# New durations and lags in a hybrid layer's ordering model, and thirteen list schedules in place of three

## The chip, the cores and the metric

The kernel runs on one core of a Trainium2 chip. The metric is the device time of one launch in microseconds (us), the median of several executions. Beside the times stands the trace of one profiled execution.

## The reference

One layer for 4096 tokens of width 1024, in float32: a pre-norm, one input projection that feeds two groups of heads, a gate on each group, one output projection, the residual and a final RMSNorm.

```python
h = _rmsnorm(x, norm_w)
u = (h @ w_in).astype(f32)                    # 1024 -> 3216 columns
# gated linear attention: 4 heads, key dim 64, value dim 128
#   S_t = diag(a_t) S_{t-1} + k_t^T v_t ;  o_t = q_t S_t        (in chunks)
gla_out = rmsnorm_of_head(o) * gla_norm_w * silu(gg)
# RWKV-7: 8 heads of size 64, token shift on r, k, v, w, a
def step(S, inp):
    r_t, w_t, k_t, v_t, kk_t, a_t = inp
    sa = jnp.einsum('bhvk,bhk->bhv', S, -kk_t)
    S = (S * w_t[:, :, None, :]
         + sa[..., None] * (kk_t * a_t)[:, :, None, :]
         + v_t[..., None] * k_t[:, :, None, :])
    y = jnp.einsum('bhvk,bhk->bhv', S, r_t)
    return S, y
rwkv_out = (group_norm(y) + bonus) * silu(rg)
merged = jnp.concatenate([gla_out, rwkv_out], axis=-1)
x = x + merged @ w_out
return _rmsnorm(x, final_norm_w)
```

## The kernel before

The 4096 tokens are worked in 8 blocks of 512. Activations lie transposed, channels on the 128 partitions and tokens along the row. The input projection's columns are 29 weight tiles of 128 columns and a narrow one; each weight and each activation is split into two float16 parts, and a projection tile (`proj`) is three products of parts over 8 tiles of depth, 24 matmuls of 512 columns into one bank of PSUM. Weights are split once, written to DRAM (`wdr`), and loaded again for each block by SyncE's queue (SP) into small rings of buffers (`wr`, `wg`, `wo` in the trace: 4, 3 and 2 buffers).

**A unit of RWKV.** The 8 heads are 4 pairs; pair times block makes 32 units. For each, `rwkv_ab` projects k, r, v and the gate, mixes in the shifted token, forms the decays, and takes the norm of k (`bones` matmuls on `rn`). Eight chunks of 64 tokens get their scores in 16 matmuls (`bank<-DD,bk`), which `copy_predicated` masks into `DD` and `Nb`. The delta rule needs the inverse of a triangular 64x64 matrix for each head and chunk. Its 32x32 diagonal blocks go through DRAM (`nd`) to a layout in which a partition holds a whole block (`f`), and 31 links of two instructions on GpSimd (POOL) invert 128 blocks at once:

```python
for j in range(31):
    m, w = j // 4 + 1, 31 - j
    E.tensor_tensor(tm[:, :m, :w], ..., ALU.mult)               # tm<-Tc,f
    E.tensor_tensor(Tc[:, :m, j + 1:], ..., tm[:, :m, :w], ALU.add)   # Tc<-Tc,tm
```

(The last unit's links run on VectorE.) The result goes back through DRAM (`td`) into `Nb`. `rwkv_i` transposes one half (`Ta`, on VectorE) and completes the 64x64 inverse by two sets of small matmuls (`bank<-Ta,Nb` is the first). `rwkv_c` then walks the state through 8 links of three matmuls (`ch<-sv,DD`, `ch<-us,Nb`, `ch<-uv,bk`) with copies by ScalarE and VectorE between them; `rwkv_d` norms and gates. The attention group runs beside this (`gla_proj`, `gla_pair`), and the output projection of a block (`out_block`, matmuls on `wo`) follows when both groups are done.

**What sets the order.** None of this is issued as it is written. Each engine is wrapped in `Engine`, and each call is recorded as a `Step` with its engine, duration, lag to its readers and what it depends on (all instructions so carry line 392 in the trace). Durations come from `cost` for VectorE ("V"), ScalarE ("S") and GpSimd ("G"), from column counts for TensorE ("T"), from bytes for DMAs ("D"). A first pass (`run`, with `account`) interleaves the streams of the program by priority and by the modelled times. Then `forward` makes a list schedule of all steps on the modelled engines, with a rank for each step; `backward` derives ranks from a schedule by going from its end to its start. `class Array` models TensorE: it charges changes of tile form, float32 passes and a slow clock after idleness. The schedules alternate, the one with the smallest modelled end is kept, and the steps are emitted in order of its start times, which gives each engine and SP's queue its order. Before, there are a first schedule, one from its ranks, and two more.

Of the kernel before, what the change touches and what calls it, by code (L numbers as in the profile page):

```python
# [25 lines left out]
SPARE = 0.45  # L26
# [55 lines left out]
def hymba_kernel(ctx, tc, xT, wt, wg, wo, wua, gup, pk, ck, out):  # L82
# [7 lines left out]
    big = ctx.enter_context(tc.tile_pool(name="big", bufs=1))  # L90
# [42 lines left out]
    class Array:  # L133
# [5 lines left out]
        def put(self, t, d, cols, tiles):  # L139
            r, c, f32 = tiles  # L140
            form = (r[1] - r[0], c[1] - c[0])
            q = [(i, j) for i in range(r[0], r[1]) for j in range(c[0], c[1])]
            turn = form != self.form
            t = max([t, self.free] + [self.tile.get(k, 0.0) for k in (self.tile if turn else q)]) + 0.09 * turn
            w, k = int(t / 3.413), self.clock
            if w > k[0]:
                k[:] = [w, 0.0, w == k[0] + 1 and k[1] >= 3060]
            k[1] += cols
            d *= 1 if k[2] else 2
            full = len(q) == 16  # L150
            if full and f32 == 2:
                d += (0.058 if cols <= 256 else 0.0) + (0.0 if self.f32 else 0.015)
            for k in q:
                self.tile[k] = t + (d if full or not f32 else 0.66 * d)
            self.form, self.f32 = form, f32 > 0
            self.free = t + (d if full or turn and f32 else d / 2 if f32 and form != (4, 1) else 0.014)
            return t, d
# [1 line left out]
    array = Array()  # L159

    def account(eng, out, ins, d, lag, cols=0, tiles=None):
        rdy = lambda k: (lambda r: r[0] - 0.1 if r[1] == eng and eng in "VSG" else r[0])(ready.get(k, (0.0, "")))
        t = max([0.0] + [rdy(k) for a in ins for k in parts(a)]
                + [used.get(k, 0.0) for k in parts(out)]
                + [rdy(k) for k in parts(out) if eng != "T"])
        if eng == "T":
            t0, d = array.put(max(t, now[0]), d, cols, tiles)
            t, now[0] = t0, array.free
        else:
            if eng == "D":  # L170
                t0 = place("H", t, 0.63)
                t = t0 + 1.28
            t = place(eng, t, d)
            if eng != "D":
                t0 = t
        for a in ins:
            for k in parts(a):
                used[k] = max(used.get(k, 0.0), t + d + (0.95 if eng == "D" else 0.1))
        for k in parts(out):
            ready[k] = (t + d + lag, eng)  # L180
        return t0

    table = [0]
    steps, wkey, rkey, wlast, readers = [], {}, {}, {}, {}
# [22 lines left out]
    def put(t0, eng, d, lag, cols, tiles, tab, outs, ins, f):  # L207

        keys = lambda aps: {k: k in {y for x in aps for y in parts(x)} for a in aps for k in whole(a)}
        ki, ko = keys(ins), keys(outs)  # L210
        for k in list(ki) + list(ko):
            t0 = max(t0, wkey.get(k, 0.0))
        for k in ko:
            t0 = max(t0, rkey.get(k, 0.0))
        s = Step(len(steps), t0, eng, d, lag, cols, tiles, tab, f)
        got = lambda m: m.lag + SPARE * (m.eng == "D") - 0.1 * (m.eng == eng and eng in "VSG")
        for k, timed in ki.items():
            rkey[k] = max(rkey.get(k, 0.0), t0)
            if k in wlast:
                s.follow(wlast[k], got(wlast[k]) if timed else None)  # L220
        for k, timed in ko.items():
            wkey[k] = t0
            if k in wlast:
                s.follow(wlast[k], got(wlast[k]) if timed and eng != "T" else None)
            for m in readers.get(k, ()):
                s.follow(m, (0.95 + SPARE if m.eng == "D" else 0.1) if timed else None)
            wlast[k], readers[k] = s, []
        for k in ki:
            if k not in ko:
                readers.setdefault(k, []).append(s)  # L230
        if eng == "T":

            if last[0] and last[1] == turn[0] and last[0].form == s.form != (4, 4):
                last[0].next = s
                s.follow(last[0], None)
            last[:] = [s, turn[0]]
        for m in s.on:
            m.to.append(s)
        steps.append(s)

    def forward(rank):


        wait, can, free = {e: [] for e in "VSGTD"}, {e: [] for e in "VSGTD"}, dict.fromkeys("VSGTDH", 0.0)
        pes, tab, run = Array(), 0, None
        left, ready, start = [len(s.on) for s in steps], [0.0] * len(steps), [0.0] * len(steps)
        end = [0.0] * len(steps)
        for s in steps:
            if not s.on:
                heapq.heappush(wait[s.eng], (0.0, s.n))  # L250

        def soonest(e):
            t = pes.free if e == "T" else free["H" if e == "D" else e]
            return t if can[e] else max(t, wait[e][0][0]) if wait[e] else 1e18

        for _ in steps:
            e = min("VSGTD", key=soonest)
            t = soonest(e)
            while wait[e] and wait[e][0][0] <= t:
                n = heapq.heappop(wait[e])[1]  # L260
                heapq.heappush(can[e], (rank[n], n))
            if e == "T":
                x = next((x for x in can[e] if run and x[1] == run.n), None)
                x = x or min(heapq.nsmallest(12, can[e]), key=lambda x: x[0] - 2.0 * (steps[x[1]].form == pes.form))
                run = steps[x[1]].next
                can[e].remove(x)
                heapq.heapify(can[e])
            else:
                x = can[e][0]
                soon = []  # L270
                while e in "VS" and wait[e] and wait[e][0][0] <= t + 0.15:
                    r, n = heapq.heappop(wait[e])
                    soon.append((r, n))
                    if rank[n] + 2 * (r - t) < x[0]:
                        x = (rank[n] + 2 * (r - t), n)
                for y in soon:
                    if y[1] != x[1]:
                        heapq.heappush(wait[e], y)
                if x is can[e][0]:
                    heapq.heappop(can[e])  # L280
            s = steps[x[1]]
            t, d = max(t, ready[s.n]), s.d
            start[s.n] = t
            if e == "T":
                start[s.n], d = pes.put(t, d, s.cols, s.tiles)
                end[s.n] = start[s.n] + d
            elif e == "D":
                free["H"], free["D"] = t + 0.63, max(t + 1.28, free["D"]) + d
                end[s.n] = free["D"]
            else:  # L290
                if s.tab is not None:
                    d, tab = d + 1.2 * (s.tab != tab), s.tab
                end[s.n] = free[e] = t + d
            for m in s.to:
                lat = m.on[s]
                ready[m.n] = max(ready[m.n], start[s.n] if lat is None or lat < 0 else end[s.n] + lat)
                left[m.n] -= 1
                if not left[m.n]:
                    heapq.heappush(wait[m.eng], (ready[m.n], m.n))
        return start, end  # L300
# [26 lines left out]
                    heapq.heappush(wait[m.eng], (ready[m.n], m.n))  # L327
        return [-t for t in late]

    def cost(eng, op, ins, n, o):  # L330

        big = [a for a in ins if math.prod(a.shape[1:]) > 1 or n == 1]
        few = len(ins) - len(big)
# [1 line left out]
        if eng == "V":  # L335
            fast = len(big) == 1 and not psum and op in ("tensor_scalar", "tensor_copy", "tensor_scalar_mul", "tensor_scalar_max")
            if op == "tensor_tensor_scan":
                return 0.068 + n / 480
            runs = 0.09 if n == 64 or len(o.shape) > 2 and o.shape[-1] == 64 and n == 512 else 0.0
            if op == "copy_predicated":  # L340
                runs = 0.09
            elif n == 256 and o.shape[0] != 128:
                runs += 0.04 if op == "transpose" else 0.09
            elif op == "tensor_scalar" and few > 1:
                runs = 0.06
            return 0.068 + 0.06 * (few > 0) + n / (1920 if fast else 960) + runs
        if eng == "G":
            return 0.225 + 0.07 * few + n * (2.13 if len(big) > 1 else 0.95) / 960
        return (0.1 if n == 64 and o.shape[0] == 64 else 0.0) + (0.052 if psum else 0.094) + n / 1200 + 0.09 * (few > 0)

    class Engine:

# [4 lines left out]
        def __getattr__(self, op):  # L357
            f = getattr(self.eng, op)

            def call(*a, **kw):  # L360
# [3 lines left out]
                if aps:  # L364
# [14 lines left out]
                    else:  # L379
                        e = kw.get("accum_out")  # L380
                        ins = [x for x in ins if x is not e]
                        outs = [o] + ([e] if e is not None else [])
                        d = cost(self.name, op, ins, n, o)
                        if op == "activation" and a[2] in (AF.Ln, AF.Exp, AF.Tanh):
                            tab = int(a[2] == AF.Ln)
                        load = 1.2 * (tab is not None and tab != table[0])
# [1072 lines left out]
    with tc.manual_schedule(engines={getattr(mybir.EngineType, e) for e in ("PE", "DVE", "Activation", "Pool", "SP")}):  # L1459
# [5 lines left out]
        run()  # L1465
        start, end = forward([s.t0 for s in steps])
        start, end = best = forward(backward(end))
        for _ in range(2):
            start, end = forward(backward(end))
            best = min(best, (start, end), key=lambda x: max(x[1]))  # L1470
        start, end = best
# [65 lines left out]
```

## Time and profile before

| | |
|---|---|
| median of 3 executions | 2358.89 us (2357.46 to 2363.66) |
| the profiled execution's own time | 2364.37 us |
| its span, first to last instruction | 2362.6 us |
| mean granted TensorE clock | 0.985 |
| DMA | 325.46 MB, mean 138 GB/s |

The page divides the span into 40 slices; a digit is the busy share of a slice in tenths.

```profile
PE   6889999999999999999999999999999999999997
DVE  6878877677764886756767678657876478676855
POOL 3351433526134152345322353332543435233400
PEclk9999999999999999999999999999999999999999
```

In the timelines a row is: start and duration in us, engine, line, operation, output and inputs by name, shape, count, and in brackets the idle time before it and what ended that.

### The profile page before, as it was taken

To read this page: it belongs to the slowest core of one execution; us is meant where nothing else is said; L and a number is where in the kernel's file an instruction comes from. 1 tells how busy PE (TensorE), PEld (TensorE's weight loads), DVE (VectorE), ACT (ScalarE), POOL (GpSimd) and SP (SyncE) were. 2 spreads that over 40 slices of the span, in tenths; PEclk is the share of its full clock that TensorE was granted. 3 is DMA by queue.
4 is the path that set the end of the run, shared out by engine and by line. 5 is a ranking of instruction groups with operands and counts; after the bars stand their busy time and mean duration, and the time that the engine had idled before them with its cause. 6 is when DMAs were issued, how large, how long until landed. Compare 5 with 4: busy or idle time off the path is not lost.

```text
span 2362.6 us, 52159 instructions
## 1 busy us (share of the span) xinstructions
PE 2250.2 (95%) x19432; PEld 1379.2 (58%) x19432; DVE 1679.0 (71%) x3737; ACT 1248.1 (53%) x3229; POOL 846.8 (36%) x2213
## 2 busy tenths in 40 slices
PE   6889999999999999999999999999999999999997
PEld 2556565556565656556575565755566556665564
DVE  6878877677764886756767678657876478676855
ACT  6557765454653554535554456445455465544442
POOL 3351433526134152345322353332543435233400
PEclk9999999999999999999999999999999999999999
DMA  6566554354334543335433444345533354334432
GB/s 190 178 217 200 186 164 153 115 169 146 100 94 142 174 150 84 110 119 182 141 96 110 152 153 133 90 124 180 152 101 106 124 183 142 97 111 124 141 82 93
DMA packets 275523, 325.46 MB, mean 138 GB/s; under 512 B 131732, under 2 KB 132932, under 8 KB 275268
## 3 DMA queue, kind: packets, MB, share of 16 engines
q1 hardware_dynamic: 275268, 322.13, 45.0%
q8 instruction: 152, 2.49, 0.4%
q14 instruction: 103, 0.84, 0.1%
HBM read 276.97 MB, written 45.05 MB: 136 GB/s over the span
## 4 chain that ended last, share of the span: by engine, by line
PE 63%; DVE 20%; ACT 6%; issue 4%; DMA 4%; POOL 3%; SPq 1%; DVEq 0%; ACTq 0%; POOLq 0%
PE bank L392 55%; PE ch L392 6%; DVE DD L392 3%; PE y L392 2%; DVE nta L392 2%; DVE bk L392 2%; DVE Nb L392 1%; POOL tm L392 1%; POOL Tc L392 1%; DVE mgg L392 1%; DVE mgr L392 1%; DMA xr<-in_xT_dram 1%; DMA rn<-bcda 1%; ACT gep L392 1%; DVE x L392 1%
## 5 line engine op out<-in xcount | busy, mean ns | idle before, releaser
L392 PE MATMUL bank<-x,wr 128*128 128x512 f16 x3264 | 806.8, 382 | 9.6 <-ACT x L392 2.8
L392 POOL TENSOR_TENSOR tm<-Tc,f 128x60 f32<-128x60 f32 (+24 forms) x961 | 332.5, 346 | 655.0 <-DMA f<-nd 535.5
L392 PEld LDWEIGHTS <-wr 128*128 128x128 f16 x3264 | 318.7, 100 | 308.0 <-issue 22.4
L392 PE MATMUL bank<-x,wg 128*128 128x512 f16 x1536 | 385.0, 381 | 5.6 <-DMA wg<-wdr 4.1
L392 POOL TENSOR_TENSOR Tc<-Tc,tm 128x60 f32<-128x60 f32 (+24 forms) x961 | 346.9, 361 | 73.7
L392 PE MATMUL bank<-x,wo 128*128 128x512 f16 x1488 | 357.0, 381 | 0.4 <-ACT bk L392 0.4
L392 DVE SCALAR_TENSOR_TENSOR sv<-ch,PC,psd 64x64 f32<-64x64 f32 x448 | 126.2, 282 | 213.4 <-PE ch L392 208.3
L392 POOL TENSOR_TENSOR xacc<-xacc,xr 128x512 f32<-128x512 f32 x98 | 130.6, 1332 | 335.4 <-ACT xr L392 237.9
L392 PEld LDWEIGHTS <-wg 128*128 128x128 f16 x1536 | 146.1, 100 | 149.7 <-issue 8.9
L392 PEld LDWEIGHTS <-wo 128*128 128x128 f16 x1488 | 144.9, 100 | 139.3 <-issue 4.1
L392 PEld LDWEIGHTS <-x 128*128 128x128 f16 x3120 | 187.5, 99 | 21.4 <-issue 6.8
L392 PE MATMUL bank<-wg,x 128*128 128x128 f16 x3072 | 196.1, 220 | 1.6 <-DMA wg<-wdr 0.8
L392 ACT ACTIVATE psd<-sv,PC 128x128 f32<-128x128 f32 x256 | 102.2, 399 | 178.3 <-DVE sv L392 139.1
L392 ACT COPY uv<-ch 64x64 f32<-64x64 f32 x512 | 105.4, 206 | 117.3 <-PE ch L392 112.5
L392 ACT COPY us<-ch 64x64 f32<-64x64 f32 x512 | 105.1, 205 | 103.8 <-PE ch L392 95.2
L392 POOL MEMSET Tc<- 32x8 f32 (+1 forms) x160 | 23.6, 148 | 302.9 <-DMA td<-Tc 280.2
L392 PEld LDWEIGHTS ch<-sv,DD 128*128 128x128 f32 x512 | 90.9, 192 | 52.1 <-DVE sv L392 25.0
L392 ACT ACTIVATE sa<-bank,mu_s 128x512 f32<-128x512 f32 x104 | 71.6, 689 | 88.7 <-PE bank L392 87.6
L392 PEld LDWEIGHTS ch<-uv,bk 128*128 128x128 f32 x512 | 90.2, 191 | 48.5 <-ACT uv L392 25.3
L392 PE MATMUL ch<-sv,DD 128*128 128x128 f32 x512 | 106.1, 289 | 12.3 <-DVE sv L392 10.9
L392 PEld LDWEIGHTS ch<-us,Nb 128*128 128x128 f32 x512 | 88.2, 192 | 44.1 <-ACT us L392 24.5
L392 PE MATMUL ch<-uv,bk 128*128 128x128 f32 x512 | 106.1, 289 | 6.3 <-ACT uv L392 5.9
(332 smaller groups left out, 3683.0 us busy)
## 6 DMA issues: line engine op xcount, KB each, us to landing
wr<-wdr SPq DMA_DIRECT2D x256, 256.0 KB
wg<-wdr SPq DMA_DIRECT2D x184, 256.0 KB
xr<-in_xT_dram SPq DMA_DIRECT2D x176, 256.0 KB
wo<-wdr SPq DMA_DIRECT2D x128, 256.0 KB
f<-nd SPq DMA_DIRECT2D x128, 128.0 KB
x<-in_wt_dram SPq DMA_DIRECT2D x29, 512.0 KB
wdr<-wo SPq DMA_DIRECT2D x25, 512.0 KB
out_dram<-mgg SPq DMA_DIRECT2D x33, 256.0 KB
```

The lines of the kernel that those rows point to most:

```text
L392: put(t0, self.name, d, lag, cols, tiles, tab, outs, ins, lambda: f(*a, **kw))
```

## The change

The code that computes is untouched; the model that orders it changes. `Array.put` charges more for a float32 matmul behind a float16 one, something for the reverse, and something for float32 matmuls of the form (2, 4). A new function `early` gives, for a pair of engines, by how much a result reaches its reader sooner than the common lag; it was 0.1 us on the same engine and nothing between engines, and is now different for each engine and pair. `cost` gets other constants for all three engines, among them GpSimd's start cost (0.225 to 0.14 us, and 0.34 more for 8 elements), half-height forms on VectorE, and short and half-height forms, several scalars and accumulation on ScalarE. A change of activation table costs 1.3 us in place of 1.2. The number of list schedules goes from 3 to 13 after the first. In the diff "V", "S", "G", "T" are VectorE, ScalarE, GpSimd, TensorE.

```diff
             if full and f32 == 2:
-                d += (0.058 if cols <= 256 else 0.0) + (0.0 if self.f32 else 0.015)
+                d += (0.058 if cols <= 256 else 0.0) + (0.0 if self.f32 else 0.045)
+            elif full and self.f32 and not f32:
+                d += 0.017
+            elif f32 and form == (2, 4):
+                d += 0.036
...
-        rdy = lambda k: (lambda r: r[0] - 0.1 if r[1] == eng and eng in "VSG" else r[0])(ready.get(k, (0.0, "")))
+        rdy = lambda k: (lambda r: r[0] + early(r[1], eng))(ready.get(k, (0.0, "")))
...
+    def early(a, b):
+        if a not in "VSGT" or b not in "VSGT" or not a:
+            return 0.0
+        if a == b:
+            return {"V": -0.075, "S": -0.1, "G": -0.18, "T": 0.0}[a]
+        return -0.045 if a == "T" else -0.09 if b == "T" else -0.07
...
-        got = lambda m: m.lag + SPARE * (m.eng == "D") - 0.1 * (m.eng == eng and eng in "VSG")
+        got = lambda m: m.lag + SPARE * (m.eng == "D") + early(m.eng, eng)
...
-                    d, tab = d + 1.2 * (s.tab != tab), s.tab
+                    d, tab = d + 1.3 * (s.tab != tab), s.tab
...
-    def cost(eng, op, ins, n, o):
+    def cost(eng, op, ins, n, o, acc=False):
...
-            runs = 0.09 if n == 64 or len(o.shape) > 2 and o.shape[-1] == 64 and n == 512 else 0.0
+            half = o.shape[0] < 128
+            runs = 0.0
             if op == "copy_predicated":
-                runs = 0.09
-            elif n == 256 and o.shape[0] != 128:
-                runs += 0.04 if op == "transpose" else 0.09
+                runs = 0.135 if half else 0.013
+            elif n == 64:
+                runs = 0.126
+            elif n == 256 and half:
+                runs = 0.122 if op == "transpose" else 0.09
+            elif n == 512 and half:
+                runs = 0.115
...
         if eng == "G":
-            return 0.225 + 0.07 * few + n * (2.13 if len(big) > 1 else 0.95) / 960
-        return (0.1 if n == 64 and o.shape[0] == 64 else 0.0) + (0.052 if psum else 0.094) + n / 1200 + 0.09 * (few > 0)
+            if op == "memset":
+                return 0.135 + n * 0.52 / 960
+            return 0.14 + 0.07 * few + n * (2.13 if len(big) > 1 else 0.95) / 960 + 0.34 * (n == 8)
+        if n <= 4:
+            return 0.1 if n == 1 else 0.03
+        if n == 64 and o.shape[0] == 64:
+            return 0.231 if psum else 0.147
+        d = (0.052 if psum else 0.094) + n / 1200 + 0.09 * (few > 0) + 0.11 * (o.shape[0] < 128)
+        return d + (0.035 + 0.05 * (few > 1) if few and psum and n > 128 else 0.02 * (few > 0)) + 0.1 * acc
...
-                        d = cost(self.name, op, ins, n, o)
+                        d = cost(self.name, op, ins, n, o, e is not None)
...
         start, end = best = forward(backward(end))
-        for _ in range(2):
+        for _ in range(12):
             start, end = forward(backward(end))
             best = min(best, (start, end), key=lambda x: max(x[1]))
```

## The prediction

> **What bounds the kernel now.** First the page: busy time, then the chain that ended last.
>
> ```profile
> PE 2250.2 (95%) x19432; PEld 1379.2 (58%) x19432; DVE 1679.0 (71%) x3737; ACT 1248.1 (53%) x3229; POOL 846.8 (36%) x2213
> PE 63%; DVE 20%; ACT 6%; issue 4%; DMA 4%; POOL 3%; SPq 1%; DVEq 0%; ACTq 0%; POOLq 0%
> ```
>
> TensorE works 2250.2 of the 2362.6 us span. No cost term and no lag changes what is computed, so that block stays: in the two compiled orders 14,756 matmul entries stand in each, and the array changes its tile form 2,139 times before and 2,141 after. Only the 2362.6 − 2250.2 = 112.4 us without TensorE work can move, and what matters is where they lie. The table by stage (columns: us of the stage, then busy us of PE, PEld, DVE, ACT, POOL, then clock, DMA share, GB/s):
>
> ```profile
> 0.00:300.00 300.00, 253.02 (x1997) 153.28 (x1997) 238.81 (x631) 195.54 (x405) 104.20 (x246) 0.95 0.62 194
> 300.00:2250.00 1950.00, 1905.07 (x16697) 1170.69 (x16695) 1374.72 (x2935) 1010.60 (x2703) 742.61 (x1967) 1.00 0.44 132
> 2250.00:2363.00 113.00, 92.09 (x745) 55.22 (x742) 65.46 (x173) 41.93 (x122) 0.00 (x0) 0.91 0.28 87
> ```
>
> The head loses 47 us, the long middle 45 (2.3%), the tail 21. Next, whom TensorE and SP's queue wait for (total, times, longest):
>
> ```profile
> PE bank L392 <- DVE bk L392: 12.9, 9, 6.8
> PE ch L392 <- DVE sv L392: 10.9, 13, 1.7
> PE bank L392 <- ACT wo L392: 6.8, 7, 2.1
> PE ch L392 <- ACT uv L392: 5.9, 11, 0.9
> PE bank L392 <- DMA wg<-wdr: 4.9, 4, 2.5
> PE bank L392 <- DVE Ta L392: 2.0, 2, 1.3
> SPq L392 <- POOL Tc L392: 101.4, 36, 6.8
> ```
>
> Many small waits, one of 6.8 us; and TensorE hardly ever waits for `Ta`, which comes out of POOL's inverse.
>
> **The change, term by term.** Every edit acts through the emitted order alone, so each is priced by what that order puts between a producer and its consumer. I compared the compiled orders of both kernels and turned the matmuls between two points into time by their columns, scaled to 2250.2 us in all. The median matmul moves 44 places of 24,516, VectorE's instructions 6, ScalarE's 5, SP's 3, POOL's 0.
>
> *Head.* The one long wait stands in TensorE's timeline:
>
> ```profile
> 59.21 0.43 PE L392 MATMUL bank<-rn,bones 128*32 128x128 f32 x8
> 59.57 4.49 PE L392 MATMUL bank<-x,wr 128*128 128x512 f16 x20
> ...
> 76.70 4.50 PE L392 MATMUL bank<-DD,bk 64*128 64x128 f32 x32 [6.82 <-DVE bk L392]
> 124.00 2.05 PE L392 MATMUL bank<-DD,bk 64*128 64x128 f32 x30 [0.27 <-DVE bk L392]
> 1007.80 2.97 PE L392 MATMUL bank<-x,wo 128*128 128x512 f16 x13
> ```
>
> From the norm sums (`rn,bones`) to the scores (`DD,bk`) lie 17.5 us, most of it a VectorE chain. The old order has 44 matmuls of 512 columns there (20 on wr, 24 on wg) and two small ones on `amW`; at 2.97/13 = 0.23 us each that is about 10 us, and then TensorE waits 6.82. In the new order the norm sums stand earlier, ahead of the low-rank matmuls, and 56 large matmuls and those small ones fill the stretch, about 12.9 us. If VectorE's chain keeps its length, the wait falls to some 2.5: −4.3. The 32 scores behind the wait took 4.50 us, 30 of a later unit 2.05; a shorter wait could give back part of these 2.3 us. Against both: 6.8 us of TensorE's waits are for `wo` still being split, and what comes sooner may wait there longer. I take −5, bounds −9 and 0. The Trainium skill ("TensorE: Matmul & The Clock Gate", § What's actually happening) says that an idle window of about 3.4 us halves the matmul clock; the 6.82 us wait with slow scores behind it agrees, and by it the whole 2.3 would come back and the term would be −6.6.
>
> *Weights.* Four weight loads have under 3 us of matmul columns between the freeing of their buffer and their first use in the old order, none in the new. The four waits for wg cost 4.9 us: −2, bounds −5 and 0.
>
> *POOL's inverse.* Here the model changes most. Each of 32 units has 31 links of two POOL instructions, and per unit the old constants (0.225, and a 0.1 lead) sum to 27.1 us, the new ones (0.14 and 0.34 for the link of 8 elements) to 22.5. The trace:
>
> ```profile
> L392 POOL TENSOR_TENSOR tm<-Tc,f 128x60 f32<-128x60 f32 (+24 forms) x961 | 332.5, 346 | 655.0 <-DMA f<-nd 535.5
> L392 POOL TENSOR_TENSOR Tc<-Tc,tm 128x60 f32<-128x60 f32 (+24 forms) x961 | 346.9, 361 | 73.7
> ```
>
> and from the timelines of POOL and VectorE, at two places:
>
> ```profile
> 517.88 0.72 POOL L392 TENSOR_TENSOR tm<-Tc,f 128x31 f32<-128x31 f32 x1 [21.93 <-DMA f<-nd]
> 519.35 0.57 POOL L392 TENSOR_TENSOR tm<-Tc,f 128x30 f32<-128x30 f32 x1
> 518.42 2.07 DVE L392 SCALAR_TENSOR_TENSOR mgr<-mgr,pkt,xacc 128x512 f32<-128x512 f32 x3
> ...
> 1005.11 0.24 POOL L392 TENSOR_TENSOR tm<-Tc,f 128x31 f32<-128x31 f32 x1 [11.46 <-DMA f<-nd]
> 1005.42 0.25 POOL L392 TENSOR_TENSOR Tc<-Tc,tm 128x31 f32<-128x31 f32 x1
> ```
>
> 31 units ran on POOL: (332.5 + 346.9)/31 = 21.9 us busy, and the starts at 1005.11 and 1005.42 leave 0.07 behind each of 62 instructions, 4.6 more: 26.5 us. The new constants are those of an undisturbed link (0.24); beside VectorE instructions with two large inputs the same link took 0.57 to 0.72. So the average chain is the old 27.1, and the new plan expects `Ta` 4.6 us too soon. The Trainium skill ("GPSIMD Engine Reference", § 1 Specifications) says that GpSimd shares its SBUF interfaces with VectorE and contends with its instructions of two SBUF inputs. The trace agrees (0.24 against 0.72), and since VectorE's work is unchanged, by this rule the mean stays at 26.5 and the plan stays short; were the rule without effect here, this term would be nothing.
>
> What that costs follows from the stretch between a unit's last score and its first `Ta` matmul:
>
> ```profile
> 231.09 1.16 PE L392 MATMUL bank<-DD,bk 64*128 64x128 f32 x16
> 282.94 0.22 POOL L392 TENSOR_TENSOR Tc<-Tc,tm 128x8 f32<-128x8 f32 x1
> ...
> 801.96 3.52 PE L392 MATMUL bank<-DD,bk 64*128 64x128 f32 x30 [0.82 <-DVE ki L392]
> 858.23 0.22 POOL L392 TENSOR_TENSOR Tc<-Tc,tm 128x8 f32<-128x8 f32 x1
> ...
> 874.56 0.43 DVE L392 STREAM_TRANSPOSE Ta<-Nb 32x256 f32<-32x256 f32 x1
> 879.18 0.69 PE L392 MATMUL bank<-Ta,Nb 32*32 32x32 f32 x32
> ...
> 2172.32 1.16 PE L392 MATMUL bank<-DD,bk 64*128 64x128 f32 x16
> 2220.94 0.22 POOL L392 TENSOR_TENSOR Tc<-Tc,tm 128x8 f32<-128x8 f32 x1
> ```
>
> Over units 2 to 30 (first and last shown, unit 10 between) POOL ends 49.7 us after the last score on average. The planned stretch is 74.3 us of TensorE work before and 70.0 after, so 24.6 remain behind POOL's end, then 20.2. Needed are two trips through DRAM and the transposes: 874.99 − 858.45 = 16.5 us at unit 10. TensorE's other waits, 45 us in 1950, add some 1.6 to each stretch of 70, so about 15 us of planned work must remain. Unit by unit, what is missing at 15 sums to 2.5 us in the old order (the trace has 2.0 on `Ta`, so 15 is about right) and to 16.2 in the new, seven units instead of one. Stalls widen few later stretches (13 of 30 overlap), so they add: +14. At 12 the sums are 0 and 3.8, at 17 they are 6.3 and 34.6: bounds 0 (POOL may also come sooner) and +28.
>
> *SP's queue.* The `td` stores wait for POOL (SP's waits for `Tc` sum to 101.4 us), and SP's queue goes out in order. In the new order the first `td` stands 6.6 us of columns earlier against the scores, so weight loads behind it go out later than their free buffers allow. Five units (2, 6, 10, 18, 22) have first uses close enough; at the 4.9/4 = 1.2 us that a late weight costs, +6, bounds 0 and 5 × 2.5 = 12.
>
> *Local waits.* Elsewhere the new constants are mostly nearer:
>
> ```profile
> L392 ACT COPY sv<-bank 64x256 f32<-64x256 f32 x128 | 46.8, 366 | 7.7 <-PE bank L392 5.8
> L392 DVE COPY_PREDICATED DD<-mc,bank 64x512 f32<-64x512 uint8 x128 | 92.3, 725 | 2.4
> L392 DVE SCALAR_TENSOR_TENSOR sv<-ch,PC,psd 64x64 f32<-64x64 f32 x448 | 126.2, 282 | 213.4 <-PE ch L392 208.3
> ```
>
> The copy is 0.265 in the old model, 0.375 in the new, 0.366 here; the predicated copy 0.691, 0.736, 0.725; but the chain's own update 0.285, 0.320, 0.282. Of the 10.9 + 5.9 us on the chain I take a fifth back, −3; a reshuffle of this size can also open waits, so −12 to +8. *Tail:* the last unit's scores stand 5 us of work later, its chain is spread more evenly, and the thin spots stay: 0, bounds −4 and +4.
>
> Sum: −5 − 2 + 14 + 6 − 3 + 0 = +10 us. The profiled execution took 2364.4 us, 5.5 over the median of 2358.9, so 2374 for it and 2369 for the median. About 0.3%, 7.1 us, is what a measurement of this kernel can tell from no change.
>
> **Rivals.** *Faster: the margin is enough.* If what must remain behind POOL is below about 12 us, the `Ta` term falls to 0, and no store goes late. For it: the old order lost only 2.0 us there, and unit 10 used 20.7 us from POOL's end to `Ta` without its row naming a wait. Against it: seven planned margins under 15, against a path of 16.5. With local waits at −8 the sum is −5 − 2 + 0 + 0 − 8 = −15: 2344.
>
> *Heavier.* The stores of `td`, standing earlier, hold SP in most units, weights come late, and the queue passes it on. At the upper bounds of both terms, −5 − 2 + 28 + 12 − 3 = +30: 2389, from about a dozen late units on. Against it: buffers are filled ahead, and only five units are close.
>
> *Nothing measurable.* The order moves a few dozen places in 24,516 and the terms cancel: `Ta` at +6, stores at +1 give about −3: 2356.
>
> **How the numbers follow.** Forecast 0.36 (2366 to 2380), heavier 0.08, nothing measurable 0.20, faster 0.36. Both signs hold much: the `Ta` term is a difference of planned sums that a few us of POOL time move across zero, while the head's gain is the best-founded single term. The range leaves out the far ends of the faster case and of the heavier one, a tenth each: 2338 to 2392. Faster by over 0.3% 0.36, within 0.20, slower 0.44.
>
> **What would show it.** Right: waits on `Ta` rise from 2.0 to some 16 us in about seven units; the wait at 76.70 shrinks under 4 us; wg waits vanish; POOL's two groups keep 346 and 361 ns. Wrong: waits on `Ta` below 5 us with the head shorter (the faster rival); or the middle stage's TensorE share below 96% with the lost time on DMAs of weights (the heavier one). Had POOL's links fallen to 0.25 on average, the step on contention would be wrong.

## The result, and the profile after

The changed kernel takes 2371.53 us (median of 11), the kernel before 2358.89 us (median of 11): ratio 1.0051, interval 1.0037 to 1.0065. It is 0.5% slower; 2369 was forecast. The profiled execution after took 2373.5 us. Its busy times, and the table by stage, of the changed kernel:

```profile
PE 2246.2 (95%) x19432; PEld 1384.1 (58%) x19432; DVE 1670.1 (70%) x3737; ACT 1249.8 (53%) x3229; POOL 853.9 (36%) x2213
```

```profile
0.00:300.00 300.00, 253.86 (x2064) 155.63 (x2064) 234.40 (x632) 196.61 (x406) 103.25 (x246) 0.94 0.62 194
300.00:2250.00 1950.00, 1893.02 (x16517) 1168.55 (x16511) 1360.38 (x2891) 1009.02 (x2696) 750.69 (x1967) 0.99 0.44 132
2250.00:2372.00 122.00, 99.32 (x862) 59.96 (x859) 75.35 (x214) 44.22 (x128) 0.00 (x0) 0.91 0.28 87
```

TensorE does the same work in 2246 us; 125.5 us of the span are without it, 112.4 before. Who it and SP's queue wait for, in the changed kernel:

```profile
PE bank L416 <- ACT wo L416: 17.9, 11, 7.1
PE ch L416 <- DVE sv L416: 16.1, 17, 2.5
PE bank L416 <- DMA wg<-wdr: 9.5, 7, 3.4
PE bank L416 <- DVE bk L416: 7.3, 10, 1.4
PE bank L416 <- DVE rgs L416: 5.9, 2, 5.2
PE bank L416 <- DVE Ta L416: 0.4, 1, 0.4
SPq L416 <- POOL Tc L416: 174.3, 39, 12.1
```

The waits on `Ta`, which the forecast rested on, did not come: 0.4 us. In their place stand waits for weights (`wo` 6.8 to 17.9, `wg` 4.9 to 9.5), one of 5.2 on `rgs`, and a longer row of SP's waits for `Tc`, 174.3 us for 101.4 before. That row holds more than the waits at the `td` stores: sorted by the transfer that each wait stands ahead of, 45.1 of the 101.4 us before and 135.5 of the 174.3 after are at `td` stores, the rest at loads of `xr`. So the standing at the stores is three times as long as before.

Both orders hold the same matmuls, so I compared the times at which the two kernels reach the same amount of matmul columns. The changed one is 5.5 us ahead after 50 us of columns and 5.9 after 90, 1.0 ahead after 130 (204 us), between 7.4 ahead and 6.0 behind with no trend through the middle, 2.5 behind at 2200 us and 8.4 behind at 2251. Two places lose: near 137 us and near 2245 us. The first, in the timelines of POOL, SP's queue, ScalarE and TensorE of the changed kernel:

```profile
129.66 0.22 POOL L416 TENSOR_TENSOR Tc<-Tc,tm 128x8 f32<-128x8 f32 x1
117.01 0.81 SPq L416 DMA_DIRECT2D wr<-wdr  x2
129.91 0.33 SPq L416 DMA_DIRECT2D td<-Tc  x1
130.33 0.40 SPq L416 DMA_DIRECT2D x<-in_wt_dram  x1
130.79 0.42 SPq L416 DMA_DIRECT2D wdr<-wo  x1
135.98 1.06 ACT L416 ACTIVATE wo<-x 128x1024 f32<-128x1024 f32 x1 [13.13 <-DMA wdr<-wo]
137.18 0.79 PE L416 MATMUL bank<-ident,amW 128*128 128x128 f32 x2 [7.09 <-ACT wo L416]
```

Read from top to bottom: POOL ends unit 0's inverse at 129.88. SP had issued its last load at 117.8 and stood for 12.1 us at the first `td` store. Behind that store were the load of a raw weight and the store of split ones; the buffer of that store is what ScalarE waits for (13.13), and TensorE waits 7.09 for ScalarE. The second place, SP, VectorE and TensorE:

```profile
2230.68 0.43 SPq L416 DMA_DIRECT2D nd<-Nb  x1
2237.18 0.30 SPq L416 DMA_DIRECT2D td<-Tc  x1
2237.59 1.11 SPq L416 DMA_DIRECT2D crs<-bcdc  x2
2241.28 0.69 DVE L416 TENSOR_TENSOR crs<-y,crs 128x512 f32<-128x512 f32 x1 [4.19 <-DMA crs<-bcdc]
...
2244.78 0.68 DVE L416 SCALAR_TENSOR_TENSOR rgs<-rgs,bank 128x512 f32<-128x512 f32 x1
2245.52 8.20 PE L416 MATMUL bank<-wg,x 128*128 128x128 f16 x96 [5.23 <-DVE rgs L416]
```

SP stands 6.1 us at a `td` store; the load of a broadcast (`crs`) goes out only behind it; VectorE stands 4.19 us for it, and the instruction that frees a bank (`rgs`) is queued behind that. TensorE waits 5.23. The two waits, 12.3 us, are about as long as the whole loss; that they are its cause is shown only by the runs below. A wait also costs something behind it: from 137.2 to 141 us the granted clock is 0.50.

### The profile page after: what moved, and what is told of

The parts are those of the page before. It is cut to its first block, busy times and chain, and to the rows that moved or that the text cites. A ratio compares the mean times of both kernels' runs of the same rounds, so it can differ in the third digit from the quotient of the medians.

```text
span 2371.7 us, 52205 instructions
## 1 busy us (share of the span) xinstructions
PE 2246.2 (95%) x19432; PEld 1384.1 (58%) x19432; DVE 1670.1 (70%) x3737; ACT 1249.8 (53%) x3229; POOL 853.9 (36%) x2213
## 4 chain that ended last, share of the span: by engine, by line
PE 63%; DVE 16%; DMA 7%; POOL 6%; ACT 3%; issue 3%; SPq 1%; DVEq 0%; ACTq 0%; POOLq 0%
PE bank L416 55%; PE ch L416 6%; POOL Tc L416 3%; POOL tm L416 3%; DVE DD L416 2%; PE y L416 2%; DVE nta L416 2%; DVE mgr L416 1%; DVE bk L416 1%; DMA wdr<-wo 1%; DMA wg<-wdr 1%; DVE mgg L416 1%; DMA f<-nd 1%; DMA rn<-bcda 1%; DVE Nb L416 1%
## 5 line engine op out<-in xcount | busy, mean ns | idle before, releaser
L416 PE MATMUL ch<-sv,DD 128*128 128x128 f32 x512 | 105.3, 288 | 16.1 <-DVE sv L416 16.1
L416 POOL MEMSET Tc<- 32x8 f32 (+1 forms) x160 | 23.9, 149 | 233.5 <-DMA td<-Tc 201.4
```

The lines of the kernel that those rows point to most:

```text
L416: put(t0, self.name, d, lag, cols, tiles, tab, outs, ins, lambda: f(*a, **kw))
```

## The experiments

All times are medians; the ratio is to runs of the kernel before on the same chip, with its interval. Theory A: the new GpSimd constants plan the `td` stores before POOL can have ended, and SP's queue, standing at them, makes other transfers late. Theory B: any new order scatters by such an amount. Theory C: the forecast's margin at `Ta`. Theory D: the number of schedules.

**GpSimd's old constants put back in the changed kernel** (`pool_old`).

```diff
-            if op == "memset":
-                return 0.135 + n * 0.52 / 960
-            return 0.14 + 0.07 * few + n * (...) / 960 + 0.34 * (n == 8)
+            return 0.225 + 0.07 * few + n * (...) / 960
...
-            return {"V": -0.075, "S": -0.1, "G": -0.18, "T": 0.0}[a]
+            return {"V": -0.075, "S": -0.1, "G": -0.1, "T": 0.0}[a]
```

> The changed kernel with GpSimd's old constants alone put back (start 0.225 us, no form of its own for memset or 8 elements, 0.1 us lead). Theory A, SP's queue: the new constants plan the td stores some 5 us before POOL ends, SP stands at them and what is queued behind comes late; then SP's waits for Tc fall from 174 us to about 100, TensorE's waits of 7.1 us (on wo, near 137) and 5.2 us (on rgs, near 2245) go, and the time comes back to 2355 to 2362. Theory B, scatter: any new order of this length falls within some 10 us and the POOL constants are not special; then 2364 to 2376 with other single waits in place of those two, whatever SP waits. Theory C, the Ta margin of the prediction: Ta waits are 0.4 us in the changed kernel, so they cannot fall, and the time stays near 2371.

2342.25 us, ratio 0.9936 (0.9919 to 0.9952): 29 us under the changed kernel and faster than the kernel before, further than theory A said. SP's row of waits fell as it said, and the part at `td` stores from 135.5 to 50.8 us (the queue's waits):

```profile
SPq L414 <- POOL Tc L414: 95.1, 37, 6.3
```

**GpSimd's new constants alone, in the kernel before** (`pool_new`): the same lines the other way, three schedules.

> The kernel before with GpSimd's new constants alone (start 0.14, memset, 8 elements, 0.18 us lead), three schedules. Theory A: SP's waits for Tc rise from 101 us to 150 or more, and the time rises by 6 to 14 us, to 2365 to 2373. Theory B: anywhere from 2352 to 2372, not tied to SP's waits. Theory C: waits on Ta rise from 2 us to 10 or more.

2390.81 us, ratio 1.0141 (1.0122 to 1.0160). The sign is A's; the size, 32 us, is more than twice the 14 that it allowed. SP's row rose to 185.5 us, 123.3 of them at `td` stores; `Ta` cost 4.0 us, so theory C is small here too (whom SP's queue and TensorE wait for):

```profile
SPq L394 <- POOL Tc L394: 185.5, 50, 11.2
PE bank L394 <- DVE bk L394: 15.7, 11, 4.1
PE bank L394 <- DMA wg<-wdr: 13.6, 6, 4.3
PE bank L394 <- DVE Ta L394: 4.0, 5, 1.9
```

**The td stores on GpSimd's queue, in the changed kernel** (`td_pool`). The model still schedules them as SP's, so the emitted order stays; only the queue that issues them differs.

```diff
             f = getattr(self.eng, op)
+            g = getattr(nc.gpsimd, op) if op == "dma_start" else None
...
-                put(t0, self.name, ..., outs, ins, lambda: f(*a, **kw))
+                put(t0, self.name, ..., outs, ins,
+                    lambda: (g if g and ins and ins[0].tensor.name.startswith("Tc") else f)(*a, **kw))
```

> The changed kernel, with the td stores issued on GpSimd's queue instead of SP's, at the same place of the emitted order; everything else is emitted as in the changed kernel. Theory A: SP waits for Tc no more, wo and rgs waits of 7.1 and 5.2 us go, 2356 to 2363. Theory B, or if the queue's wait only stands for a late POOL: the time stays at 2367 to 2374, since POOL ends no sooner. A cost of issuing 128 stores on POOL may lengthen its chain by a few us per unit.

2341.06 us, ratio 0.9924 (0.9909 to 0.9939): 30 us less with the same order, twice the most that theory A gave and far outside B's range. This is the run that decides: every engine and SP's queue get the same instructions in the same order, the 128 stores apart. The same places in its trace (SP, VectorE, TensorE), and POOL's groups:

```profile
121.20 0.33 SPq L418 DMA_DIRECT2D x<-in_wt_dram  x1
121.58 0.43 SPq L418 DMA_DIRECT2D wdr<-wo  x1
...
2206.76 0.68 DVE L418 TENSOR_TENSOR crs<-y,crs 128x512 f32<-128x512 f32 x1
2210.99 5.18 PE L418 MATMUL bank<-wg,x 128*128 128x128 f16 x90 [0.94 <-DVE rgs L418]
```

```profile
L418 POOL TENSOR_TENSOR Tc<-Tc,tm 128x60 f32<-128x60 f32 (+24 forms) x961 | 347.4, 362 | 74.3
L418 POOL TENSOR_TENSOR tm<-Tc,f 128x60 f32<-128x60 f32 (+24 forms) x961 | 331.3, 345 | 757.6 <-DMA f<-nd 559.6 <-DMA wr<-wdr 53.3 <-DMA bv<-bcdb 38.8
L418 POOL DMA_DIRECT2D td<-Tc x128 | 75.2, 593 | 39.1 <-issue 30.2 <-POOL Tc L418 8.7
```

The raw weight is loaded at 121.20, not 130.33; the wait of 7.09 is gone and that of 5.23 is 0.94. POOL's links are no faster, and POOL ends a unit's inverse no sooner: 47.8 us behind the unit's last score in the changed kernel and 47.5 here, on average over units 2 to 30. Nor is it the stores' own earlier landing, since TensorE waited only 0.4 us for `Ta` before the move. Compared by columns, the profiled execution gains on that of the changed kernel (2335.0 us of span for 2371.7) in steps: 9.9 us near 137 us, some 16 more up to 456, 5 near 830, 7 near 2240, and little between. So SP's standing also cost where no single large wait shows it, above all in the first 480 us. Part of the gain is in busy time: the same matmuls take 2234.4 us, 11.8 less than in the changed kernel, at a mean granted clock of 0.987 for 0.981:

```profile
PE 2234.4 (96%) x19432; PEld 1376.1 (59%) x19432; DVE 1672.9 (72%) x3737; ACT 1250.1 (54%) x3229; POOL 923.4 (40%) x2341
```

**The same move in the kernel before** (`td_before`).

> The kernel before, with the td stores issued on GpSimd's queue at the same place of the emitted order. SP waits 101 us for Tc there, against 174 us in the changed kernel, where the same move gained 30 us. If SP's standing costs in proportion (theory A): 30 x 101/174 = 17 us, so 2338 to 2348. If the standing costs only beyond what the plan of the old constants allows for (theory A2): 2354 to 2360.

2350.65 us, ratio 0.9965 (0.9952 to 0.9979): 8 to 10 us, between the two ranges.

**With GpSimd's old constants in the changed kernel, and the same move** (`both`):

> The changed kernel with GpSimd's old constants put back and the td stores on GpSimd's queue. If the store's wait is all that the constants matter for, this equals the changed kernel with the stores moved: 2335 to 2345. If old constants (2342, SP waits 95 us) and moved stores add up: 2326 to 2334.

2335.97 us, ratio 0.9904 (0.9889 to 0.9920), the lowest median of all and 6 to 8 us under `pool_old`. It lies in the first range, and its interval overlaps that of `td_pool`: the two moves don't add up, and a remaining worth of the constants with the stores moved (5 us by the medians) is at the edge of the noise.

The expectation of 17 us for `td_before` took SP's whole row of waits for `Tc` as standing at the stores. With the stores gone from SP's queue, the row still shows (`td_pool`, `td_before`, `both`):

```profile
SPq L418 <- POOL Tc L418: 39.2, 12, 6.0
SPq L394 <- POOL Tc L394: 55.1, 19, 5.7
SPq L416 <- POOL Tc L416: 47.8, 17, 4.7
```

What left the queue is 174.3 − 39.2 = 135 us, 101.4 − 55.1 = 46 and 95.1 − 47.8 = 47. Moving the stores is worth 30 us where SP stood 135 us at them, 8 to 10 at 46, and 6 to 8 at 47: 30 × 46/135 = 10 us, so in these two orders the gain goes with the standing at the stores; `both` gains somewhat less than its 47 us would give.

**The number of schedules.** The changed kernel with 3 instead of 13 (`three`), the kernel before with 13 (`before13`), and the changed kernel with GpSimd's old constants and 3 (`pool_old3`):

```diff
-        for _ in range(12):
+        for _ in range(2):
```

> The changed kernel with 3 list schedules instead of 13, all new constants kept. Theory A: SP's waits for Tc stay above 140 us and the time within 2364 to 2376. If the ten further schedules carry the difference (theory D), the time falls to 2360 or below.

> The kernel before with 13 list schedules and nothing else changed. If the number of schedules carries the gain that the changed kernel has with GpSimd's old constants (2342): 2338 to 2350. If the other new constants carry it: 2354 to 2362. With the new GpSimd constants, going from 3 to 13 schedules was worth 2387 - 2371 = 16 us.

> The changed kernel with GpSimd's old constants and 3 list schedules, that is, the kernel before with the other new constants (TensorE, VectorE, ScalarE, lags, table load). If the schedules carry the gain: 2354 to 2364. If these constants do: 2338 to 2350. If neither alone and the two only work together, both this and the kernel before with 13 schedules stay above 2352.

2387.04 (ratio 1.0122, 1.0101 to 1.0143), 2358.92 (0.9994, 0.9981 to 1.0008) and 2343.31 us (0.9932, 0.9918 to 0.9945). Where the plan is near the truth, ten more schedules do nothing: 2359 either way, 2343 or 2342. With the new GpSimd constants they took 16 us away (`three` lies above both of its ranges), so theory D holds only there. The other new constants are worth −16 to −18 us with three schedules (`pool_old3`).

**GpSimd's lead alone put back** (`lead`: `"G": -0.18` to `"G": -0.1`).

> The changed kernel with GpSimd's lead alone put back from 0.18 to 0.1 us. Each of the 62 instructions of an inverse is then planned 0.08 us longer: the plan of the chain goes from 62 x (0.14 + 0.02) + 6.9 + 0.7 = 17.5 us to 22.5; the old constants plan 27.1, the trace shows about 26.5. If the loss goes in proportion to how much too early the plan is (9.0 us too early: 2371; right: 2342): 4 us too early gives 2355, bounds 2350 to 2361, SP's waits for Tc near 135 us. If only the start constant matters (0.14 in place of 0.225), the time stays above 2364.

2376.67 us, ratio 1.0073 (1.0058 to 1.0088): the expectation of 2355 fell, and the time lies where it was to stay if the start constant alone mattered. SP's row is still 160.5 us, 117.6 of them at `td` stores, and TensorE's waits on `wo` are larger than in the changed kernel:

```profile
PE bank L416 <- ACT wo L416: 24.8, 13, 9.4
```

A plan of 22.5 us for the inverse is as bad as one of 17.5; the loss is not in proportion to the error. **A plan that is too long** (`over`: GpSimd's old constants, `0.225` to `0.295`):

> The changed kernel with GpSimd's old constants and 0.07 us more for each start: the inverse is planned at 31.4 us, 5 us longer than it takes. If SP's standing for Tc still costs at 95 us: it falls to 50 to 70 us and the time to 2332 to 2340. If the right duration is best: 2342 or more, with TensorE's work on the units bunched later; 2342 to 2352.

2388.08 us, ratio 1.0127 (1.0113 to 1.0141), above both ranges. SP stands less (78.8 us in the row, 17.1 at `td` stores behind POOL, and one wait of 15.1 us at the last unit's, behind VectorE), and here, with room planned for a slower POOL, TensorE waits for `Ta` and for the last unit's inverse, which runs on VectorE:

```profile
PE bank L414 <- DVE Ta L414: 13.2, 9, 5.5
PE bank L414 <- DVE Tc L414: 4.2, 1, 4.2
```

The 17.4 us of these two waits (2.6 in `pool_old`) explain part of the 46 us over `pool_old`; where the rest went stays open. So the standing at the stores is not all that a wrong duration costs.

**The other constants, in two halves**, each in the kernel before with 3 schedules: VectorE's and ScalarE's durations (`durs`), and lags, TensorE terms and table load (`lags`), each being the lines of the change that bear on them.

> The kernel before with the new durations of VectorE and ScalarE alone (3 schedules, old GpSimd constants, old lags and TensorE terms). All new constants but GpSimd's gained 16 us together. If these durations carry it: 2340 to 2350. If not: 2354 to 2364.

> The kernel before with the new lags between engines (GpSimd's own lead kept at 0.1), the TensorE terms and the table load alone (3 schedules, old durations). The complement of the run with the durations: if lags and TensorE terms carry the 16 us: 2340 to 2350; if not: 2354 to 2364; if each half gives a part, both lie between 2345 and 2355.

2349.07 us (0.9961, 0.9947 to 0.9975) and 2380.84 us (1.0097, 1.0084 to 1.0111); both halves together are `pool_old3` at 2343. They don't add: −9, +23, together −16 to −18. `lags` lies outside all of its ranges. SP's row of waits for `Tc` is 136.0 us in `durs`, which is faster than the kernel before, and 120.9 in `lags`; at `td` stores behind POOL it is 60.6 and 46.8, so the row as a whole doesn't rank these kernels. With the new lags and the old, shorter durations, TensorE waits more on the chain (`lags`; these three are 33.2 us, in `durs` 9.9 + 2.3 + 3.4):

```profile
PE ch L404 <- DVE sv L404: 12.5, 16, 2.3
PE ch L404 <- ACT us L404: 12.2, 21, 3.2
PE ch L404 <- ACT uv L404: 8.5, 14, 1.9
```

That fits lags and durations that were fitted together and are right only as a sum; it was not tested further. Theory B keeps a part: orders from similar models differ by tens of us.

## Why the prediction was right, and where it was not

The time and the sign were right, 2371.5 for 2369, but by luck: two errors cancel, +14 for a term that came to nothing and +6 for one of some +21. Two kernels with the stores moved tell the terms apart: without SP's standing at the stores, the new order is 0.41% faster than the old (0.9924 against 0.9965), −10 us. That is head, weights and local waits together, and their forecasts sum to −10. The standing costs 30 us after and 8 to 10 before: +20 to +22. That these add up to the measured difference follows from how they are taken, from the same four times; what the runs show is how it divides. By its own signs the forecast's mechanism failed: waits on `Ta` of 0.4 us with the head shorter were to speak for the faster rival, and the middle stage's TensorE share of 97% (1893.02 of 1950 us) not for the heavier one; neither sign looked at SP's queue.

One premise was not exact: that only the 112.4 us without TensorE work can move. The same matmuls were busy from 2234.4 us (`td_pool`, granted clock 0.987) to 2259.4 (`three`, 0.978).

- *Head, −5: right.* The wait of 6.82 us is gone and the scores start 7.0 us sooner (TensorE's timeline of the changed kernel):

```profile
69.67 2.52 PE L416 MATMUL bank<-DD,bk 64*128 64x128 f32 x32
```

  The 32 scores took 4.50 us behind the wait, at a granted clock of 0.50, and 2.52 without it, at 1.00. The rule of the Trainium skill ("TensorE: Matmul & The Clock Gate", § What's actually happening), by which an idle window halves the matmul clock, gave −6.6 with all of that returned; the trace agrees with the rule, and the −5.9 at 90 us of columns lies between the two forecasts. The caution that what comes sooner may wait for `wo` came true at 137 us, for a reason that was not named there.
- *Weights, −2: wrong sign in the changed kernel.* Waits on `wg` rose from 4.9 to 9.5. Counting columns between a freed buffer and its first use leaves out that SP may stand when the buffer is free. With the stores moved, the same waits nearly vanish in both orders (`td_pool`, then `td_before`):

```profile
PE bank L418 <- DMA wg<-wdr: 0.4, 1, 0.4
PE bank L394 <- DMA wg<-wdr: 1.0, 1, 1.0
```

- *POOL's inverse, +14: wrong, in two places.* The lead of 0.18 was left out: the new plan is 62 × (0.14 + 0.02) + 6.9 + 0.7 = 17.5 us, not 22.5, and 9 us short, not 4.6. That didn't enter the +14, which was counted in the compiled orders. The step that failed there is the need of 15 us behind POOL's end, which is no constant. Over units 2 to 30, from POOL's end to the end of the first transpose it was 20.7 us before and 17.0 after, down to 11.1, and POOL itself ended 1.7 us sooner behind the last score. `Ta` waits came to 0.4 us. The stores explain little of the shorter trip: the first one goes out 0.9 us behind POOL's end before and 0.1 after, and with the stores moved the trips are still 20.5 (`td_before`) and 16.4 us (`td_pool`). The trip goes with the emitted order of what follows the stores, the loads into `Nb` and the transposes; why just these places moved stays open. What stayed right is that POOL itself doesn't change: 346 and 361 ns a link before, and in the page's groups after

```profile
L416 POOL TENSOR_TENSOR tm<-Tc,f 128x60 f32<-128x60 f32 (+24 forms) x961 | 336.6, 350 | 711.2 <-DMA f<-nd 540.8
L416 POOL TENSOR_TENSOR Tc<-Tc,tm 128x60 f32<-128x60 f32 (+24 forms) x961 | 346.5, 361 | 74.3
```

  350 and 361 after, as the rule on SBUF interfaces shared with VectorE in the Trainium skill ("GPSIMD Engine Reference", § 1 Specifications) had it for unchanged VectorE work.
- *SP's queue, +6: the mechanism that decided, at under a third of its size.* The 101.4 us named there are not all at the stores (45.1 are), so the rise, to 135.5, was steeper than the row shows. Only weights behind the stores were counted. The largest victims were the stores and raw loads of weight splitting and a broadcast, which free buffers and banks elsewhere.
- *Local waits, −3, and tail, 0.* The chain's waits on `sv` rose from 10.9 to 16.1 us in the changed kernel. With the stores moved, its waits on `sv`, `uv` and `us` are 23.9 us in the new order and 18.3 in the old, so the chain gave nothing back; of the −10 above, the head's part is shown and the rest is not assigned. From 2200 us on the chain's waits rose by 1.8 us (6.5 to 8.3), and 5.2 more are the wait on `rgs`.

The rival "faster" (2344) would have been the result had the stores not stood in SP's queue: 2341 with its `Ta` term at nothing, as it assumed, though not with the gain in local waits that it counted on. The "heavier" one named the right mechanism with too wide a reach.

## What to carry to other kernels

In an order planned by a model, price a wrong duration at every in-order queue that waits for the result, not only at its consumer: here the consumer lost 0.4 us and the queue some 20. A store that waits for a slow producer belongs on the producer's own queue; that one move was worth 6 to 30 us in three orders, and with it the new GpSimd constants cost some 5 us, at the edge of the noise, instead of 29. When a queue's waits are summed by what ended them, sort them also by the transfer that they stand ahead of: here over half of the sum before was not at the stores. Constants that were fitted together (durations and lags, typical and disturbed) should be tried together and one by one, since each half can be worse than none.

## What the runs showed of the hardware

A store issued by GpSimd took 0.59 us of its queue (75.2 us for 128), and the links of the inverse were as fast beside it (345 and 362 ns). The stores issued by GpSimd landed a median 2.7 us after issue in `td_before` and in `td_pool`, where the trace tells the landing. The trip of the inverse from POOL to the transposed operand took 20.7 us on average in the kernel before, and 20.5 in `td_before`, where a unit's four stores were out 4.0 us behind POOL's end in place of 8.8: the first load back went out 11.6 and 10.8 us behind POOL's end. So a good part of what looked like DMA latency was the place of the loads and the transposes in the order.
